# A down projection in four groups of four chunks with seven block products in place of eight

## The chip, the core and the metric

The kernel runs on one core of one Trainium2 chip. The metric is the device time of one execution in microseconds. A core has TensorE (PE, its weight loads as PEld), VectorE (DVE), ScalarE (ACT), GpSimd (POOL) and SyncE (SP), which issues the DMAs. TensorE writes to the eight banks of PSUM.

## What is computed

One layer of a hybrid decoder on 512 tokens of width 1024, all in fp32. The part that matters here is the channel mixer, whose hidden width is 2816, or 22 chunks of 128 channels:

```python
hf = rmsnorm(x, norm_ffn[i])
up = causal_dwconv(hf @ w_up[i], ffn_dw_w[i], ffn_dw_b[i])
gate, val = jnp.split(up, 2, axis=-1)
x = x + (jax.nn.gelu(gate) * val) @ w_down[i]
```

Ahead of it stand a convolution and a sparse attention over a combined projection, merged and projected; behind it a gated embedding and a last norm.

## The kernel before

Every fp32 operand of a large product is cut into a pair of parts, hi (a ScalarE copy, `hi_of`, L107) and lo (a VectorE subtraction, `lo_of`, L110). A product takes three matmuls: hi with hi, hi with lo, lo with hi (L117 to L119 with the weight as stationary operand, L123 to L125 with the activations).

**Weights** come as a stream of 512 KB pieces in their order of use (`pieces`, `Stream`). SyncE loads a piece into one of two buffers (L208); `pump`, which each consumer calls once a piece, starts the cut of pieces that were asked for in an earlier call, up to four pieces ahead (`CUT`). The stages of a cut are put between the matmuls by `work`, so that they stand at a fixed place in the queues of ScalarE and VectorE.

**The channel mixer** goes through the 22 chunks in groups of 8, 8 and 6 (`FFN_GROUPS`). For each chunk f, `up_chunk` (L1161) runs 24 matmuls for the gate half and 24 for the value half, with 128 channels on the partitions and 512 tokens as columns. Behind each half come the depthwise convolution's first tap on ScalarE (L1170) and two on VectorE (L1171, L1172); behind the gate half the gelu (L1180); behind the value half the multiplication (L1182) and the cut of the result into the stationary parts `a` (L107, L110). Then `rows_product` multiplies the group's chunks by w_down: for each column half n and each pair of chunks it takes one piece of weights and runs 4 row tiles of 128 tokens with 2 chunks and 3 matmuls each, into four banks that stay open over the group. At the end of a half, VectorE adds the four banks to the residual `x2` (`residual`, L1137). The chunk pairs come in order, so the chunk that was ready last is used last.

Each engine works its queue in program order, and a DMA queue does too. Nothing but the order of the program and buffers (eight banks of `ps`, eight tiles tagged `act`, four `whl`) decides when something runs.

Of the kernel before, what the change touches and what calls it, by code (L numbers as in the profile page):

```python
# [16 lines left out]
P = 128  # L17
# [24 lines left out]
# heads whose scores, two units ahead, and whose weights, one unit ahead, are due in a unit's steps  # L42
# [41 lines left out]
def block_kernel(ctx: ExitStack, tc: tile.TileContext, x, p, rel_bias, norm_mix, w_in, conv_dw_w, conv_dw_b,  # L84
# [30 lines left out]
    # out += W.T a  with W's parts as the stationary operand  # L115
# [5 lines left out]
    # out += a.T W  with the activations' parts as the stationary operand  # L121
    def mm_a(o, a_hi, a_lo, w_hi, w_lo, start, stop):
        nc.tensor.matmul(o, a_hi, w_hi, start=start, stop=False)  # L123
        nc.tensor.matmul(o, a_hi, w_lo, start=False, stop=False)  # L124
        nc.tensor.matmul(o, a_lo, w_hi, start=False, stop=stop)  # L125

# [1 line left out]
    # A piece lands as fp32 and is cut into an exact (hi, lo) pair of float32r parts, some pieces ahead of its use.  # L128
# [24 lines left out]
    CMP_AFTER = CMP_AT                      # the compression's eight pieces follow the z pieces from this one on  # L153
# [10 lines left out]
    FFN_GROUPS = ((0, 8), (8, 16), (16, NF))  # L164
    for f0, f1 in FFN_GROUPS:
        for f in range(f0, f1):
            for c in (f, NF + f):
                pieces.append((("up", c), [cols(w_up, 0, KC, c * P, P)], KC, P, "whl"))
        if f1 == NF:
            ple_piece(1)  # L170
        rows_pieces("down%d" % f0, w_down, list(range(f0, f1)))
# [4 lines left out]
    class Stream:  # L176
# [6 lines left out]
        def pump(self, force=False):  # L183
            """asks for the next pieces; starts to cut those that were asked for in an earlier call"""
            while self.stages:
                self.work()
            while self.cuts < self.dmas and (force or self.asked[self.cuts] < self.call):
                i = self.cuts
                key, _, a, b, tag = pieces[i]
                if tag is not None:  # L190
                    if tag == "whl" and self.hls >= self.limit:
                        break
                    hl = work("whl", (P, 2, a, b), F32R, tag=tag, bufs=CUT if tag == "whl" else 1)
                    self.hl[i] = hl
                    self.cut(hl, self.raw[i], a)
                    self.hls += tag == "whl"
                    self.raws -= 1
                self.cuts += 1
            while self.dmas < len(pieces):
                i = self.dmas  # L200
                key, srcs, a, b, tag = pieces[i]
                if (self.wholes if tag is None else self.raws) == 2:
# [12 lines left out]

        def cut(self, hl, raw, a):
            """in stages, so that neither engine waits for the other"""
            n = self.parts
            ks = [slice(a * j // n, a * (j + 1) // n) for j in range(n)]
            for j in range(n + 1):  # L220
                def stage(j=j):
                    if j < n:
                        hi_of(hl[:, 0, ks[j]], raw[:, ks[j]])
                    if j:
                        lo_of(hl[:, 1, ks[j - 1]], raw[:, ks[j - 1]], hl[:, 0, ks[j - 1]])
                self.stages.append(stage)
            self.work()
# [18 lines left out]

        def done(self):
# [4 lines left out]

    st = Stream()

# [13 lines left out]
    VNG = ((0, 3), (3, 3), (6, 2))          # row blocks of the values' and branch gates' weights  # L268
# [29 lines left out]
    for _ in range(WARM):                  # keeps the tensor engine's clock up until the first rows are there  # L298
# [3 lines left out]
    class Norm:  # L302
        """RMS norm of one row tile, whose halves may come one after the other."""
# [32 lines left out]
        def to_T(self, hT, t):  # L336
            """-> hT[:, part, kc, tokens]"""
# [9 lines left out]
    def vec_rows(name, parts):  # L347
        """parts: list of [r, 128] APs stacked on partitions -> [128, sum r]."""
# [52 lines left out]
    # relative bias: W[q, h, j] = -bias_h(384 + q - j), +BIG where the distance is negative  # L401
# [7 lines left out]
    # the first tile's norm is shared out, as everything waits for it  # L409
# [75 lines left out]
    KQ = work("KQ", (P, 2, 2, NG, S), F32R, tag="B", bufs=2)   # [(dup d), branch, part, group, token]  # L485
    QQ = work("QQ", (P, NH, S), F32R, tag="B", bufs=2)         # [(part d), head, token]
# [48 lines left out]
    def kpe_evac(kv, o):  # L535
        """the windows' first (ab = 0) and second halves: k[s] + pe[16 ab + s % 16]"""
# [7 lines left out]
    def cmp_x(kv):  # L544
        """Xw[kv][ab][(r d), g, s] = kpe[(g d), s + r]"""
# [68 lines left out]
    def conv_steps():  # L614
        while len(conv_done) < 4 * (CONV_W - 1):
# [3 lines left out]
            # two chains take turns; an instruction then follows one that it doesn't wait for  # L619
# [9 lines left out]
    def conv_tail():  # L629
        """layer norm over channels (on transposed rows), then silu(x) = x/2 (1 + tanh(x/2))"""  # L630
# [71 lines left out]
    def pv_mm(po, v, a, n, start, stop):  # L702
        """po += [v_hi | v_lo].T @ (probabilities, hi and lo part)."""
# [30 lines left out]
    class Unit:  # L734
        """softmax weights of four heads (a group) over one branch's keys, for a tile of queries"""

        def __init__(self, t, g, b):
# [3 lines left out]
            per = min(HPG, 512 // self.nk)              # heads in a tile of 512  # L741
# [78 lines left out]
    def attention(order):  # L820
# [3 lines left out]
        def step(place, fn=None):  # L824
            """one step of the pipeline; fn is run a step later"""
# [7 lines left out]
        def ahead(i):  # L833
            """opens unit i"""
# [65 lines left out]
    class Pace:  # L900
        """runs steps of a generator at a rate, until it ends"""
# [142 lines left out]
    # per-layer embedding rows: p^T parts  # L1044
# [33 lines left out]

# [1 line left out]
    def rows_product(name, ks, a_of, done, late=None, filler=None, between=None, last=None):  # L1080
        """for every row tile t and column half n: done(t, n, psum of a.T @ w[:, half]);
        late(t): what follows a row tile's second half, on the tensor engine after the next tile's product."""
        for n in range(2):
            o = [ps() for _ in range(NT)]
# [61 lines left out]

    gain_f = load_gain(norm_ffn)
    hfT = work("hfT", (P, 2, KC, S), F32R, tag="A", bufs=1)
    hl_ple = st.take("ple", 0)
    for t in range(NT):  # L1150
# [4 lines left out]
                 lambda t: norms[t].to_T(hfT, t), lambda: ple_half(0, hl_ple))  # L1155

# [17 lines left out]

    hpT = gain_p = None
    for f0, f1 in FFN_GROUPS:
        act = {}
# [10 lines left out]
        if f1 < NF:  # L1188
            rows_product("down%d" % f0, ks, a_of, lambda t, n, o: residual(t, n, o, None))
        else:  # L1190
            gain_p = load_gain(norm_ple)
            hpT = work("hpT", (P, 2, KC, S), F32R, tag="A", bufs=1)
            st.pump()
            hl_ple1 = st.take("ple", 1)
            rows_product("down%d" % f0, ks, a_of, lambda t, n, o: residual(t, n, o, gain_p),
                         lambda t: norms[t].to_T(hpT, t), lambda: ple_half(1, hl_ple1))

# [6 lines left out]
    def gate(t, c0, c1, o):  # L1204
        """x2 += sigmoid(o) * ple; ple holds half of it, and sigmoid(x) = (1 + tanh(x/2)) / 2"""
# [21 lines left out]
    def gate_last(hls, o):  # L1227
        """the last tile's second half in two parts, so that less follows the last product"""
# [55 lines left out]
```

## Time and profile before

| what | value |
|---|---|
| median of 3 runs | 837.25 us (836.99 to 838.62) |
| span of the profiled execution | 835.6 us |
| PE busy | 821.3 us, 98% |
| PEld busy | 669.0 us, 80% |
| DVE busy | 539.6 us, 65% |
| ACT busy | 375.4 us, 45% |
| POOL busy | 24.7 us, 3% |
| DMA, mean over the span | 101 GB/s |

The profiled execution's own time is given as its span alone, from its first to its last instruction; the median run is 1.65 us longer, which is what lies around a span. Busy time is the union of an engine's instructions. Matmuls overlap in a pipeline, so the duration of one is longer than its distance to the next; the distance is what a matmul costs. In a timeline row the first two numbers are start and duration, and the brackets at its end hold the engine's idle time before it and what ended it.

### The profile page before, as it was taken

To read this page: it belongs to the slowest core of one execution; us is meant where nothing else is said; L and a number is where in the kernel's file an instruction comes from. 1 tells how busy PE (TensorE), PEld (TensorE's weight loads), DVE (VectorE), ACT (ScalarE), POOL (GpSimd) and SP (SyncE) were. 2 spreads that over 40 slices of the span, in tenths; PEclk is the share of its full clock that TensorE was granted. 3 is DMA by queue.
4 is the path that set the end of the run, shared out by engine and by line. 5 is a ranking of instruction groups with operands and counts; after the bars stand their busy time and mean duration, and the time that the engine had idled before them with its cause. 6 is when DMAs were issued, how large, how long until landed. Compare 5 with 4: busy or idle time off the path is not lost.

```text
span 835.6 us, 10144 instructions
## 1 busy us (share of the span) xinstructions
PE 821.3 (98%) x3872; PEld 669.0 (80%) x3872; DVE 539.6 (65%) x907; ACT 375.4 (45%) x677; POOL 24.7 (3%) x71
## 2 busy tenths in 40 slices
PE   7999999999999999999999999999999999999996
PEld 6888888888888886888788888888888888888885
DVE  6379977988987897935566663355654356655564
ACT  6332524287778874432544441234442123433443
POOL 2000000000010000001000000000000000001012
PEclk9999999999999999999999999999999999999999
DMA  7347787411110116430333324232333323341312
GB/s 217 83 112 202 165 188 173 96 51 51 51 51 27 51 52 219 134 101 26 100 101 102 93 85 125 80 94 81 99 100 102 101 75 102 102 147 55 120 32 101
DMA packets 108026, 84.54 MB, mean 101 GB/s; under 512 B 4080, under 2 KB 93608, under 8 KB 107978
## 3 DMA queue, kind: packets, MB, share of 16 engines
q1 hardware_dynamic: 107978, 83.90, 35.5%
q8 instruction: 30, 0.49, 0.3%
q14 instruction: 18, 0.15, 0.1%
HBM read 79.36 MB, written 2.43 MB: 98 GB/s over the span
## 4 chain that ended last, share of the span: by engine, by line
PE 96%; ACT 1%; DVE 1%; DMA 1%; issue 0%; POOL 0%; SPq 0%; POOLq 0%; ACTq 0%
PE ps L117 19%; PE ps L119 19%; PE ps L118 19%; PE ps L123 9%; PE ps L124 9%; PE ps L125 9%; PE ps L759 2%; PE ps L785 2%; PE ps L565 2%; PE ps L704 1%; PE ps L705 1%; PE ps L341 1%; PE ps L713 1%; DMA vraw<-in_w_in 1%; PE ps L803 0%
## 5 line engine op out<-in xcount | busy, mean ns | idle before, releaser
L110 DVE TENSOR_TENSOR whl<-wraw,whl 128x1024 fp32r<-128x1024 f32 (+1 forms) x159 | 155.6, 987 | 146.8 <-ACT whl L107 143.7
L107 ACT ACTIVATE whl<-wraw 128x1024 fp32r<-128x1024 f32 (+1 forms) x159 | 133.7, 862 | 124.2 <-PE ps L125 94.3
L117 PE MATMUL ps<-hfT,whl 128*128 128x512 f32 x352 | 139.1, 395 | 0.3 <-ACT hfT L107 0.3
L118 PE MATMUL ps<-hfT,whl 128*128 128x512 f32 x352 | 139.1, 395 | 0.2 <-DVE hfT L110 0.2
L119 PE MATMUL ps<-hfT,whl 128*128 128x512 f32 x352 | 139.0, 395 | 0.0
L117 PE MATMUL ps<-hT,whl 128*128 128x512 f32 x256 | 102.8, 402 | 0.0
L119 PE MATMUL ps<-hT,whl 128*128 128x512 f32 x256 | 101.1, 395 | 0.3 <-DVE whl L110 0.3
L118 PE MATMUL ps<-hT,whl 128*128 128x512 f32 x256 | 100.9, 394 | 0.0
L625 DVE SCALAR_TENSOR_TENSOR acc<-aT,convw,acc 128x512 f32<-128x512 f32 x120 | 86.2, 746 | 1.0
L118 PEld LDWEIGHTS ps<-hfT,whl 128*128 128x128 f32 x352 | 66.2, 188 | 16.4 <-DVE hfT L110 0.5
L117 PEld LDWEIGHTS ps<-hfT,whl 128*128 128x128 f32 x352 | 66.2, 188 | 16.2 <-ACT hfT L107 0.5
L119 PEld LDWEIGHTS ps<-hfT,whl 128*128 128x128 f32 x352 | 66.2, 188 | 15.9
L123 PE MATMUL ps<-whl,a 128*128 128x512 f32 x176 | 69.7, 396 | 0.0
L125 PE MATMUL ps<-whl,a 128*128 128x512 f32 x176 | 69.5, 395 | 0.0
L124 PE MATMUL ps<-whl,a 128*128 128x512 f32 x176 | 69.5, 395 | 0.0
L1170 ACT ACTIVATE up<-ps,ffnw 128x512 f32<-128x512 f32 x44 | 34.3, 780 | 61.5 <-PE ps L119 61.5
L1171 DVE SCALAR_TENSOR_TENSOR up<-ps,ffnw,up 128x511 f32<-128x511 f32 x44 | 33.0, 750 | 43.9 <-ACT up L1170 43.8
L119 PEld LDWEIGHTS ps<-hT,whl 128*128 128x128 f32 x256 | 48.2, 188 | 12.0 <-DVE whl L110 0.7
L117 PEld LDWEIGHTS ps<-hT,whl 128*128 128x128 f32 x256 | 48.2, 188 | 9.9 <-issue 0.2
L118 PEld LDWEIGHTS ps<-hT,whl 128*128 128x128 f32 x256 | 48.3, 189 | 9.4
L125 PEld LDWEIGHTS ps<-whl,a 128*128 128x128 f32 x176 | 33.0, 188 | 8.0
L123 PEld LDWEIGHTS ps<-whl,a 128*128 128x128 f32 x176 | 33.1, 188 | 7.9
(191 smaller groups left out, 1263.6 us busy)
## 6 DMA issues: line engine op xcount, KB each, us to landing
wraw<-in_w_up SPq DMA_DIRECT2D x44, 512.0 KB
wraw<-in_w_in SPq DMA_DIRECT2D x32, 512.0 KB
wraw<-in_w_down SPq DMA_DIRECT2D x22, 512.0 KB
wraw<-in_w_out SPq DMA_DIRECT2D x8, 512.0 KB
wraw<-in_w_ple_gate SPq DMA_DIRECT2D x8, 512.0 KB
W<-vdram SPq DMA_DIRECT2D x8, 264.0 KB
xin<-in_x SPq DMA_DIRECT2D x4, 512.0 KB
wraw<-in_w_ck SPq DMA_DIRECT2D x4, 512.0 KB
```

The lines of the kernel that those rows point to most:

```text
L107: nc.scalar.activation(dst, src, AF.Copy, scale=scale)
L110: nc.vector.tensor_tensor(dst, src, f32(hi), op=ALU.subtract)
L117: nc.tensor.matmul(o, hl[:, 0, j, cs], a_hi, start=start, stop=False)
L118: nc.tensor.matmul(o, hl[:, 0, j, cs], a_lo, start=False, stop=False)
L119: nc.tensor.matmul(o, hl[:, 1, j, cs], a_hi, start=False, stop=stop)
L123: nc.tensor.matmul(o, a_hi, w_hi, start=start, stop=False)
L124: nc.tensor.matmul(o, a_hi, w_lo, start=False, stop=False)
L125: nc.tensor.matmul(o, a_lo, w_hi, start=False, stop=stop)
L565: nc.tensor.matmul(hid_ps[kv][hf], raw[:, jj, hf * P:(hf + 1) * P], Xw[kv][j // 8][:, :, s0:s0 + 16 * (NCMP - 1) + 1:16], start=j == 0, st ...
L625: nc.vector.scalar_tensor_tensor(acc[:, c, :], a[:, k:k + S], convw[:, 4 * k + c:4 * k + c + 1], acc[:, c, :], op0=ALU.mult, op1=ALU.add)
L1170: nc.scalar.activation(u, o, AF.Identity, scale=fw(2, c), bias=fw(3, c))
L1171: nc.vector.scalar_tensor_tensor(u[:, 1:], o[:, :S - 1], fw(1, c), u[:, 1:], op0=ALU.mult, op1=ALU.add)
```

## The change

Sixteen of the 22 chunks are now worked in four groups of four; the last group of six is as before. In a group of four the product is taken as two pairs of chunks. For a pair, the activations are a 2 by 2 matrix of blocks (256 tokens by 128 channels) and the weights are one too (128 channels by 512 columns). Seven block products stand in place of eight, by a form of Strassen's scheme that works on sums and differences of blocks.

- `act_pair` collects the two multiplied chunks of a pair in `apair`. GpSimd makes four sums of 256 columns (s1, s3, s2, s4); then ScalarE and VectorE cut four tiles into parts: blocks 11 and 12 (512 columns), block 22 (256), s1 and s3 (512), s2 and s4 (512).
- `Quad` loads a group's four weight blocks (4 DMAs of 512 KB, issued behind the group's last up piece) into one buffer of tag `B`. GpSimd makes the differences t1, t2, t3 (`sums`) and t4 (`last_sum`), 1024 columns each. Seven operands are cut for four chunks, where before four chunks took four pieces.
- `seven_products` runs seven products of 2 row tiles, 2 pairs and 3 matmuls. The first (bank pair m) is copied by ScalarE into a second bank pair, `seeded`, that stays taken from the product with w_out to the last group of four; `seeded` then gathers three more products, and a third pair e takes two. VectorE adds a bank pair to `x2` six times in a group.
- In each product both pairs of chunks are used, the second right behind the first.

```diff
-    FFN_GROUPS = ((0, 8), (8, 16), (16, NF))
+    FFN_GROUPS = ((0, 4), (4, 8), (8, 12), (12, 16), (16, NF))
+    DOWN_OPS = ("11", "t1", "t2", "21", "t3", "22", "t4")
...
+    class Quad:
+        def __init__(self, f0):
+            raw = work("draw", (P, 4, 2, 512), tag="B", bufs=2)
...
+                nc.sync.dma_start(raw[:, i], rows[:, r, :, c * 512:(c + 1) * 512])
...
+        def sums(self):
+            x = work("dsum", (P, 2, 2, 512), tag="accX")
+            self.at["t1"], self.at["t2"], self.at["t3"] = x[:, 0], x[:, 1], self.at["12"]
+            self.sub(x[:, 0], "12", "11")
+            self.sub(x[:, 1], "22", "t1")
+            self.sub(self.at["12"], "22", "12")
+        def last_sum(self):
+            self.at["t4"] = self.at["11"]
+            self.sub(self.at["11"], "21", "t2")
...
+    def act_pair():
+        raw = work("apair", (P, 2, 512), tag="pT", bufs=2)
+        for j in range(2):
+            uv = yield
+            nc.vector.tensor_tensor(raw[:, j], uv[0], uv[1], op=ALU.mult)
...
+        add = lambda to, a, b, op: nc.gpsimd.tensor_tensor(to, a, b, op=op)
+        add(s1, a21, a22, ALU.add)
+        add(s3, a11, a21, ALU.subtract)
+        add(s2, s1, a11, ALU.subtract)
+        add(s4, a12, s2, ALU.subtract)
+        parts = {}
+        for src, names in ((raw[:, :, 0:256], ("11", "12")), (a22.unsqueeze(1), ("22",)), (sums[0], ("s1", "s3")),
+                           (sums[1], ("s2", "s4"))):
+            n = len(names)
+            x_ = work("a", (P, 2, n, 256), F32R, tag="act", bufs=8)
+            hi_of(x_[:, 0], src)
+            lo_of(x_[:, 1], src, x_[:, 0])
...
+        def product(bank, a, b, start):
+            st.pump()
+            hl = st.take("down", f0, b)
+            for tt in range(2):
+                ts = slice(tt * P, (tt + 1) * P)
+                for i, pair in enumerate(pairs):
+                    mm_a(bank[tt], pair[a][:, 0, ts], pair[a][:, 1, ts], hl[:, 0, i, :], hl[:, 1, i, :],
+                         start and i == 0, i == len(pairs) - 1, skip_group_check=True)
+                st.work()
+            st.done()
+        m, e = [ps(), ps()], [ps(), ps()]
+        product(m, "11", "11", True)
+        for tt in range(2):
+            nc.scalar.activation(seeded[tt], m[tt], AF.Copy)
+        product(e, "s1", "t1", True)
+        product(seeded, "s2", "t2", False)
+        add_to(1, 1, e)
+        add_to(0, 1, seeded)
+        product(m, "12", "21", False)
+        add_to(0, 0, m)
+        product(seeded, "s3", "t3", False)
+        add_to(1, 1, seeded)
+        product(e, "s4", "22", False)
+        add_to(0, 1, e)
+        product(seeded, "22", "t4", False)
+        add_to(1, 0, seeded)
```

Two places of the order are shown, both at a group's end. In the rows, `ps` is a bank, `whl` a weight's parts, `a` the parts of activations, `hfT` the up projection's input, and a number behind a name tells buffers apart.

TensorE before, behind the last up chunk of the first group of eight, where `a_3823` and `a_3896` are the group's first two chunks:

```order
L119 MATMUL ps_4303<-hfT_3348,whl_4191 128x512
L123 MATMUL ps_4337<-whl_4226,a_3823 128x512 [waits Activation_49]
L124 MATMUL ps_4337<-whl_4226,a_3823 128x512 [waits DVE_49]
L125 MATMUL ps_4337<-whl_4226,a_3823 128x512
L123 MATMUL ps_4337<-whl_4226,a_3896 128x512
L124 MATMUL ps_4337<-whl_4226,a_3896 128x512
L125 MATMUL ps_4337<-whl_4226,a_3896 128x512
L123 MATMUL ps_4338<-whl_4226,a_3823 128x512
```

TensorE with the change, behind the last up chunk of the first group of four, where `a_3905` holds the first pair's blocks 11 and 12 and `a_4063` those of the second pair:

```order
L119 MATMUL ps_4026<-hfT_3350,whl_3918 128x512
L123 MATMUL ps_4075<-whl_3957,a_3905 128x512 [waits Activation_49]
L124 MATMUL ps_4075<-whl_3957,a_3905 128x512 [waits DVE_49]
L125 MATMUL ps_4075<-whl_3957,a_3905 128x512
L123 MATMUL ps_4075<-whl_3957,a_4063 128x512 [waits Activation_49]
L124 MATMUL ps_4075<-whl_3957,a_4063 128x512
L125 MATMUL ps_4075<-whl_3957,a_4063 128x512 [waits DVE_49]
L123 MATMUL ps_4076<-whl_3957,a_3905 128x512
```

The fourth matmul behind the last up chunk now uses the parts of the pair that this up chunk belongs to; before, it used those of the group's second chunk of eight.

ScalarE with the change at the same place, from the last up chunk's first tap (L1231, L1170 of before) to the first cut behind the copies (`asums` are GpSimd's sums of the second pair, `draw` the weights as loaded, and L1284 the copies into the seeded banks):

```order
L1231 ACTIVATE up_4052<-ps_4026,ffnw1_820 128x512 [waits PE_49]
L107 ACTIVATE a_4063<-apair_3917 128x512 [waits DVE_49]
L107 ACTIVATE a_4066<-apair_3917 128x256
L107 ACTIVATE a_4069<-asums_4057 128x512 [waits Pool_49]
L107 ACTIVATE a_4072<-asums_4058 128x512 [waits Pool_49]
L107 ACTIVATE whl_4079<-draw_3828 128x1024 [waits DMAHW1_49]
L1284 ACTIVATE ps_3346<-ps_4075 128x512 [waits PE_49]
L1284 ACTIVATE ps_3347<-ps_4076 128x512 [waits PE_49]
L107 ACTIVATE whl_4096<-draw_3828 128x1024
```

Before, one cut of `a` stood there and cuts of weights behind it; now two cuts that wait for GpSimd stand ahead of the copies into the seeded banks.

## Rows read from the trace of the kernel before

**Rows 1.** The page: span, and part 1's busy time by engine.

```profile
span 835.6 us, 10144 instructions
PE 821.3 (98%) x3872; PEld 669.0 (80%) x3872; DVE 539.6 (65%) x907; ACT 375.4 (45%) x677; POOL 24.7 (3%) x71
```

**Rows 2.** The page, part 4: the chain that ended last, by engine.

```profile
PE 96%; ACT 1%; DVE 1%; DMA 1%; issue 0%; POOL 0%; SPq 0%; POOLq 0%; ACTq 0%
```

**Rows 3.** Busy us in stretches: 16 up chunks, then the first product.

```profile
core 0: us, PE busy (x) PEld busy (x) DVE busy (x) ACT busy (x) POOL busy (x), PEclk, DMA share, GB/s
404.92:494.00 89.08, 89.08 (x383) 72.26 (x384) 53.36 (x62) 38.28 (x48) 0.00 (x0) 1.00 0.33 95
494.00:538.60 44.60, 44.60 (x193) 35.87 (x192) 17.16 (x19) 9.78 (x10) 0.00 (x0) 1.00 0.34 104
```

**Rows 4.** Timeline, TensorE where the first product begins: start us, duration us.

```profile
494.02 0.40 PE L123 MATMUL ps<-whl,a 128*128 128x512 f32 x1
...
494.71 0.39 PE L123 MATMUL ps<-whl,a 128*128 128x512 f32 x1
...
495.41 0.40 PE L123 MATMUL ps<-whl,a 128*128 128x512 f32 x1
```

**Rows 5.** The same timeline on ScalarE and VectorE, behind the last up chunk.

```profile
494.22 0.78 ACT L1170 ACTIVATE up<-ps,ffnw 128x512 f32<-128x512 f32 x1 [1.55 <-PE ps L119]
...
495.03 0.75 DVE L1171 SCALAR_TENSOR_TENSOR up<-ps,ffnw,up 128x511 f32<-128x511 f32 x1 [1.10 <-ACT up L1170]
...
495.81 0.75 DVE L1172 SCALAR_TENSOR_TENSOR up<-ps,ffnw,up 128x510 f32<-128x510 f32 x1
...
496.60 0.69 DVE L1182 TENSOR_TENSOR up<-up 128x512 f32<-128x512 f32 x1
...
497.32 0.63 ACT L107 ACTIVATE a<-up 128x512 fp32r<-128x512 f32 x1 [2.33 <-DVE up L1182]
...
497.99 0.69 DVE L110 TENSOR_TENSOR a<-up,a 128x512 fp32r<-128x512 f32 x1 [0.70 <-ACT a L107]
```

**Rows 6.** Timeline, TensorE after a wait for a part.

```profile
404.92 0.51 PE L118 MATMUL ps<-hfT,whl 128*128 128x512 f32 x1 [0.23 <-DVE hfT L110]
...
405.26 0.39 PE L119 MATMUL ps<-hfT,whl 128*128 128x512 f32 x1
```

**Rows 7.** Groups by line and shape from 430 us on.

```profile
L110 DVE TENSOR_TENSOR whl<-wraw,whl 128x1024 fp32r<-128x1024 f32 x68 | 83.2, 1224 | 106.0 <-ACT whl L107 105.9
...
L107 ACT ACTIVATE whl<-wraw 128x1024 fp32r<-128x1024 f32 x68 | 71.3, 1051 | 85.0 <-PE ps L125 84.1 <-DMA wraw<-in_w_down 1.0
...
L1137 DVE TENSOR_TENSOR x<-ps,x 128x512 f32<-128x512 f32 x24 | 16.1, 686 | 7.6 <-PE ps L125 7.6
...
L1133 ACT ACTIVATE ple<-ps 128x512 f32<-128x512 f32 x4 | 2.2, 608 | 0.3 <-PE ps L125 0.3
```

**Rows 8.** The same view: a VectorE addition of 256 columns.

```profile
L1209 DVE TENSOR_TENSOR x<-x,pg 128x256 f32<-128x256 f32 x2 | 0.8, 424 | 0.1
```

**Rows 9.** Groups of POOL over the whole span.

```profile
L327 POOL TENSOR_TENSOR rstd<-ss 128x1 f32<-128x1 f32 x16 | 5.7, 353 | 54.1 <-ACT junk L314 53.4 <-ACT junk L1242 0.7
...
L607 POOL MEMSET aT<- 128x30 f32 x4 | 0.4, 116 | 64.8 <-DVE acc L625 64.8
...
L509 POOL MEMSET KCt<- 128x128 f32 x1 | 0.2, 205 | 0.0
```

**Rows 10.** Stretches behind the last matmul, columns as in rows 3.

```profile
828.00:832.00 4.00, 0.00 (x0) 0.00 (x0) 2.40 (x6) 2.05 (x6) 1.37 (x3) 1.00 0.34 126
...
832.40:832.60 0.20, 0.00 (x0) 0.00 (x0) 0.00 (x0) 0.00 (x0) 0.00 (x0) 0.53 0.00 0
```

**Rows 11.** Timeline, TensorE in the first stage: matmuls of 280 columns.

```profile
12.35 0.43 PE L123 MATMUL ps<-vhl,hT 128*128 128x280 f32 x1
...
12.58 0.43 PE L124 MATMUL ps<-vhl,hT 128*128 128x280 f32 x1
```

More of the change, by code (lines that the diff above doesn't have):

```diff
@@ L170, in block_kernel @@
             ple_piece(1)
-        rows_pieces("down%d" % f0, w_down, list(range(f0, f1)))
+        if f1 < NF:
+            quad_pieces(f0)
+        else:
+            rows_pieces("down%d" % f0, w_down, list(range(f0, f1)))
     rows_pieces("gate", w_ple_gate, list(range(KC)))
@@ L189, in pump @@
                 key, _, a, b, tag = pieces[i]
-                if tag is not None:
+                if tag == "quad":
+                    quads[key[1]].sums()
+                elif tag == "op":
+                    if self.hls >= self.limit:
+                        break
+                    hl = work("whl", (P, 2, a, b), F32R, tag="whl", bufs=CUT)
+                    self.hl[i] = hl
+                    self.cut(hl, quads[key[1]].at[key[2]], a)
+                    if key[2] == "11":
+                        self.stages.append(quads[key[1]].last_sum)
+                    self.hls += 1
+                elif tag is not None:
                     if tag == "whl" and self.hls >= self.limit:
@@ L1077, in block_kernel, with rows_product @@
             nc.vector.scalar_tensor_tensor(yT[m][:, 1], ysum[m], 0.5, f32(yT[m][:, 0]), op0=ALU.mult, op1=ALU.subtract)
-    def rows_product(name, ks, a_of, done, late=None, filler=None, between=None, last=None):
+    def rows_product(name, ks, a_of, done, late=None, filler=None, between=None, last=None, banks=None):
         for n in range(2):
-            o = [ps() for _ in range(NT)]
+            o = [banks[t] if n and banks and t < len(banks) else ps() for t in range(NT)]
             def part(t, kk, hl):
@@ L1145, in residual @@
             norms[t].rows()
+    seeded = [ps(), ps()]
     gain_f = load_gain(norm_ffn)
@@ L1154, in block_kernel @@
                  lambda t, n, o: residual(t, n, o, gain_f),
-                 lambda t: norms[t].to_T(hfT, t), lambda: ple_half(0, hl_ple))
+                 lambda t: norms[t].to_T(hfT, t), lambda: ple_half(0, hl_ple), banks=seeded)
     def fw(k, c):
@@ L1173, in up_chunk @@
         return u
+    def act_pair():
[3 more added lines that the diff above has]
+            nc.vector.tensor_tensor(raw[:, j], uv[0], uv[1], op=ALU.mult)
+        sums = [work("asums", (P, 2, 256), tag="S", bufs=8) for _ in range(2)]
+        a11, a21, a12, a22 = (raw[:, j, h * 256:(h + 1) * 256] for j in range(2) for h in range(2))
+        s1, s3, s2, s4 = sums[0][:, 0], sums[0][:, 1], sums[1][:, 0], sums[1][:, 1]
+        add = lambda to, a, b, op: nc.gpsimd.tensor_tensor(to, a, b, op=op)
[10 more added lines that the diff above has]
+            lo_of(x_[:, 1], src, x_[:, 0])
+            for i, name in enumerate(names):
+                parts[name] = x_[:, :, i]
+        yield parts
@@ new lines, in seven_products, with add_to @@
+    def seven_products(f0, pairs):
+        x_ = lambda r, c, tt: x2[:, 2 * r + tt, c * 512:(c + 1) * 512]
+        def add_to(r, c, bank):
+            for tt in range(2):
+                nc.vector.tensor_tensor(x_(r, c, tt), bank[tt], x_(r, c, tt), op=ALU.add)
+        def product(bank, a, b, start):
[10 more added lines that the diff above has]
+        product(m, "11", "11", True)
+        for tt in range(2):
+            nc.scalar.activation(seeded[tt], m[tt], AF.Copy)
[11 more added lines that the diff above has]
+        add_to(1, 0, seeded)
@@ L1175, in block_kernel @@
     hpT = gain_p = None
     for f0, f1 in FFN_GROUPS:
+        if f1 < NF:
+            pairs = []
+            for f in range(f0, f1, 2):
+                pair = act_pair()
+                next(pair)
+                for j in range(2):
+                    ug = up_chunk(f + j)
+                    nc.scalar.activation(ug, ug, AF.Gelu_apprx_tanh)
+                    uv = up_chunk(NF + f + j)
+                    parts = pair.send((ug, uv))
+                pairs.append(parts)
+            st.skip("quad", f0)
+            seven_products(f0, pairs)
+            continue
@@ L1187, in block_kernel @@
         a_of = lambda k, t: (act[k][:, 0, t * P:(t + 1) * P], act[k][:, 1, t * P:(t + 1) * P])
[L1188 to L1196, printed above, removed]
+        gain_p = load_gain(norm_ple)
+        hpT = work("hpT", (P, 2, KC, S), F32R, tag="A", bufs=1)
+        st.pump()
+        hl_ple1 = st.take("ple", 1)
+        rows_product("down%d" % f0, ks, a_of, lambda t, n, o: residual(t, n, o, gain_p),
+                     lambda t: norms[t].to_T(hpT, t), lambda: ple_half(1, hl_ple1))
     gain_o = load_gain(norm_final)
```

28 lines of the change are left out of this document (24 added, 4 removed).

## The prediction

> **What bounds the kernel now.** I read the page's busy shares first, then the chain that ended last, then stretches of the channel mixer, then single rows at the one place where the change alters what TensorE waits for. TensorE is busy for 821.3 of 835.6 us [rows 1] and makes up 96% of the chain that ended last [rows 2]. In the channel mixer it has no hole at all: it is busy for the whole of the 16 up chunks (89.08 us, so 5.57 us a chunk) and for the whole of the first product (44.60 us), while VectorE is busy for 17.16 us of that product, ScalarE for 9.78 and GpSimd for none [rows 3]. So here a matmul less is time less, and any wait of TensorE is time more.
>
> What is a matmul worth? Not its recorded 0.40 us, as these overlap. Six matmuls lie between the starts at 494.02 and 495.41 [rows 4], 0.232 us each, and 44.60 us for the product's 192 matmuls [rows 3] gives the same.
>
> **What the change takes away.** Sixteen chunks took two groups of 192 matmuls, 384. Now each of four groups runs 7 products x 2 row tiles x 2 pairs x 3 matmuls = 84, together 336. That is 48 less: 48 x 0.232 = 11.1 us saved, if nothing else changes.
>
> **What it adds on the path: a wait at each group's start.** Before, a product began with the group's first chunks, and the chunk just finished was used last, over 60 matmuls later. Now the fourth matmul of the first product needs the parts of the second pair, which the last up chunk has only just delivered. How long these parts take can be read off, because the same chain ran before beside the product [rows 5]: first tap on ScalarE from 494.22, second and third tap on VectorE from 495.03 and 495.81, the multiplication from 496.60, hi from 497.32 for 0.63, so until 497.95, lo from 497.99 until 498.68. The new pair tile changes none of these sizes: the tile cut first has 512 columns too. ScalarE and VectorE are idle ahead of this chain in the row (1.55 and 1.10 us), and the change puts nothing more there.
>
> TensorE by these times: three matmuls on the first pair from 494.02, then nothing. The fourth starts when hi is there, at 497.99. A matmul that ends such a wait pushes the next one back: after a wait the distance was 0.34 us (404.92 to 405.26 [rows 6]) in place of 0.232. So the fifth starts at 498.33, the sixth waits for lo until 498.72, and the seventh starts at 499.06, where before the seventh of the product started at 495.41 [rows 4]. The delay is 3.65 us a group, 14.6 us in four.
>
> **What it adds beside the path.** Counted from that start, products two to seven begin at 500.45, 503.2, 506.0, 508.8, 511.6 and 514.4, 2.78 us each.
>
> ScalarE's queue behind hi: the cut of block 22, two cuts of GpSimd's sums, the cut of a weight, two copies into the seeded banks, which the third product needs at 503.2. The copies wait behind the cut of s2 and s4, which waits for four GpSimd sums of 256 columns. No row has such a sum on GpSimd. Below, it is bounded by VectorE's addition of 256 columns, 0.42 us [rows 8]; above, by GpSimd's own addition of one column, 0.353, and three streams of 256 columns at the pace of its memsets, (205 - 116) / 98 columns = 0.9 ns a column [rows 9]: 0.353 + 3 x 0.23 = 1.05 us. I take 0.75, the middle, since neither end is nearer in kind. From the multiplication's end at 497.3, four of them end at 500.45; then 0.63 for the cut, 1.05 for the weight's and 0.61 for a copy [rows 5, 7], which overlap by some 0.07 at each change: the first copy is done at 502.65, 0.55 ahead of need. The cover is gone at 0.90 us a sum, and at 1.05 the third product starts 0.6 us late. The sums s1 and s3, which the second product's fourth matmul needs at 501.15, are early by 1.5 us.
>
> VectorE's queue has no idle time left in a group: behind lo of the pair 0.42 + 2 x 0.69 for the other cuts, seven cuts of weights at 1.22 and twelve additions at 0.69 [rows 5, 7, 8], 18.6 us in 19.5. Step by step, the addition that empties the first seeded bank ends at 508.84, where the fifth product wants that bank at 508.8. So this train runs level with TensorE, and any lateness of it comes through. I charge 0.2 us a group, between 0 (the train as reckoned) and 1.0 (three further links of 0.3).
>
> The weights' differences are off the path: 16 GpSimd additions of 1024 columns, at most 0.353 + 3 x 0.93 = 3.1 us each by the same bound, three of them, 9.4 us, spread over the last three up chunks, 16.7 us. Their loads (four blocks of 512 KB a group, on SyncE's queue ahead of the next group's up pieces) are issued some three chunks, 16.7 us, ahead of the first cut and five, 28 us, ahead of the last; at 104 GB/s [rows 3] the up piece ahead of them and the first block take 10 us, all four 25 us. The three extra cuts a group and the two seeded banks, which leave six for the rest, cost nothing while the up chunks hide them, as VectorE is busy for 53.36 of 89.08 us there [rows 3].
>
> **Sum.** 4 x (3.65 + 0.2) - 11.1 = 15.4 - 11.1 = 4.3 us longer: a span of 839.9 us for 835.6. The median run stands 1.65 us above the profiled span, so I forecast 841.5 us.
>
> **Rivals.**
>
> *GpSimd and VectorE get in each other's way.* While the four sums run, VectorE makes lo of the pair and of block 22 from two SBUF inputs each. No row has GpSimd on more than one column beside such work: it is idle in both stretches [rows 3]. If they take turns, lo of the pair takes 0.69 us longer, on the path: 2.8 us in four groups, 844.3. If GpSimd's chain and VectorE's train slip by 1.1 us more, 4.4 us come on top, 848.7. It decides from a sum of 0.90 us on, or from any lengthening of lo. The Trainium skill speaks for it: "GPSIMD Engine Reference", section "Key points", says that GpSimd shares its SBUF interfaces with VectorE and contends with VectorE instructions that have two SBUF inputs. No run here shows it so far.
>
> *TensorE's clock falls during the wait.* The wait is 3.3 us of idle TensorE. At the end of the kernel the granted clock was still 1.00 over the four idle us from 828 to 832 and had fallen by 832.4 [rows 10], which is 4.5 us behind the last matmul, so the wait should be too short. At the lower level a matmul of 280 columns took 0.23 us (12.35 to 12.58 [rows 11]), the price of 512 columns later, so about half speed. If a wait cost as much again in slow running, half of 3.4 us, four groups would cost 6.8 us: 848.3. The Trainium skill, "TensorE: Matmul & The Clock Gate", section "Part 1: The HAM clock gate", says that idle time sets the clock back to 1.2 GHz; by the row above the trace agrees for a longer gap.
>
> *Faster: a matmul is worth its duration.* If each of the 48 matmuls gave back its recorded 0.40 and not 0.232 us, 19.2 us would go and 15.4 come: 833.4. It decides from 15.4 / 48 = 0.32 us a matmul. Rows 3 and 4 speak against it.
>
> *No change that can be told.* If the wait were 2.4 to 3.2 us a group, as when one of the six links overlaps another by 0.5 to 1.2 us, the sum lies within 1.7 us of zero, about 837.3. Nothing in the rows shows such an overlap, as each link reads what the one before wrote.
>
> **How the numbers follow.** About 0.2% (1.7 us) is what a measurement of this kernel can tell from no change. Chances: the forecast 0.64 (840.7 to 844, from no charge for VectorE's train to sums at their upper bound), the contention 0.14, the clock 0.06, the duration 0.05, no change 0.11. Faster by over 0.2% is the duration's 0.05, the same is 0.11, slower 0.84. The predicted time is the forecast's, 841.5. The range reaches from 838.7, which leaves out the faster case and most of the unchanged one (0.15), to 848.0, which takes in the contention but for its worst end and leaves out the clock.
>
> **What would show it.** TensorE should have four idle gaps of about 3.3 us each, one behind the last up chunk of each group of four, ended by ScalarE's cut of `a`; the distance of matmuls should stay 0.232 us and the granted clock 1.00. The chain that ended last should hold ScalarE and VectorE, at the lines of the taps, the multiplication and the cut, for some 14 us more. GpSimd's sums of 256 columns should take 0.4 to 1.05 us. I would be wrong if the gaps were shorter than 2.8 us (then the product savings win), if TensorE waited for GpSimd or for the seeded banks by over 0.6 us a group, or if lo of the pair took more than 0.75 us.

## The result and the profile after

The changed kernel took 860.53 us (median of 4 runs, 859.85 to 860.86), the kernel before, run beside it on the same chip, 837.12 (836.97 to 838.62): a ratio of 1.0272 [1.0258, 1.0287]. The two medians lie 23.4 us apart; the ratio makes it 22.8 us, and the shares below go by the ratio. The forecast was 4.3 us longer, with a range up to 848.0. The direction was right, the size was off by a factor of five.

The page of the kernel after: span, TensorE's busy time, the granted clock in 40 slices, the chain that ended last by engine, and the group of the first matmul of a product (out<-in, count, busy, mean ns, idle before it and its releaser).

```profile
span 859.1 us, 10235 instructions
...
PE 819.0 (95%) x3824; PEld 666.3 (78%) x3824; DVE 600.7 (70%) x967; ACT 397.2 (46%) x713; POOL 98.9 (12%) x119
...
PEclk9999999999999999999998998999899899999998
...
PE 82%; DVE 8%; ACT 3%; issue 2%; POOL 2%; DMA 1%; SPq 0%; POOLq 0%; ACTq 0%
...
L123 PE MATMUL ps<-whl,a 128*128 128x512 f32 x160 | 67.5, 422 | 24.8 <-ACT a L107 24.8
```

Against [rows 1] TensorE runs 48 matmuls less, as planned, but is busy for only 2.3 us less, and the span is 23.5 us longer. In the chain, TensorE's 96% [rows 2] became 82%; VectorE, ScalarE and GpSimd hold 13%. The 24.8 us of idle time are four waits of 6.2 to 6.3 us, one at the start of each group's products, ended by the cut of `a`. That is the place that the prediction named, at nearly twice the idle time that it gave (3.3 us). And the clock row, which should have stayed at 9, has an 8 wherever such a wait lies (the last 8 is the kernel's end).

The timeline of the kernel after, at one group's end (start us, duration us; idle time and what ended it in brackets):

```profile
450.97 0.40 PE L125 MATMUL ps<-whl,a 128*128 128x512 f32 x1
...
453.39 0.76 ACT L1231 ACTIVATE up<-ps,ffnw 128x512 f32<-128x512 f32 x1
...
454.66 0.74 DVE L1232 SCALAR_TENSOR_TENSOR up<-ps,ffnw,up 128x511 f32<-128x511 f32 x1
455.44 0.75 DVE L1233 SCALAR_TENSOR_TENSOR up<-ps,ffnw,up 128x510 f32<-128x510 f32 x1
456.22 0.69 DVE L1243 TENSOR_TENSOR apair<-up 128x512 f32<-128x512 f32 x1
456.95 0.94 ACT L107 ACTIVATE a<-apair 128x512 fp32r<-128x512 f32 x2 [2.79 <-DVE apair L1243]
456.99 1.90 POOL L1247 TENSOR_TENSOR asums<-apair 128x256 f32<-128x256 f32 x2 [8.30 <-DVE apair L1243]
...
457.63 0.80 PE L123 MATMUL ps<-whl,a 128*128 128x512 f32 x1 [6.26 <-ACT a L107]
458.22 0.63 PE L124 MATMUL ps<-whl,a 128*128 128x512 f32 x1
458.65 0.63 PE L125 MATMUL ps<-whl,a 128*128 128x512 f32 x1
...
461.64 0.49 PE L123 MATMUL ps<-whl,a 128*128 128x512 f32 x1
461.97 0.40 PE L124 MATMUL ps<-whl,a 128*128 128x512 f32 x1
```

From the second tap (454.66) to the cut (456.95), the links and their lengths are those of [rows 5]. But the chain starts late. In [rows 5] the second tap stands 1.01 us behind the start of the first product (495.03 against 494.02); here the first product began at 450.51, so the tap was due at 451.52 and came 3.14 us later. Then, behind the wait, matmuls start 0.43 us apart in place of 0.232, from 458.22 to 461.64.

Stretches of the kernel after around that wait, columns as in [rows 3] (TensorE's clock stands behind POOL's busy time):

```profile
454.50:455.00 0.50, 0.00 (x0) 0.00 (x0) 0.50 (x2) 0.00 (x0) 0.00 (x0) 1.00 0.00 0
455.00:455.50 0.50, 0.00 (x0) 0.00 (x0) 0.46 (x2) 0.00 (x0) 0.00 (x0) 0.51 0.00 0
461.00:461.50 0.50, 0.50 (x2) 0.40 (x2) 0.00 (x0) 0.50 (x2) 0.00 (x0) 0.50 0.00 0
462.00:462.50 0.50, 0.50 (x4) 0.41 (x3) 0.30 (x1) 0.50 (x2) 0.00 (x0) 1.00 0.00 0
```

TensorE had stood idle since 451.4 when the granted clock fell to its lower level (1.2 GHz) at about 455.0, inside the wait; it was back at the upper one by 462.0, with four us of matmuls in between.

So there are two questions: where the chain lost 3.1 us, and what the clock costs. The first is answered half a group earlier. The timeline of the kernel after on GpSimd, VectorE and ScalarE, behind the group's fourth up chunk:

```profile
435.49 2.40 POOL L298 TENSOR_TENSOR dsum<-draw 128x1024 f32<-128x1024 f32 x1
435.56 0.63 ACT L107 ACTIVATE a<-asums 128x512 fp32r<-128x512 f32 x1 [1.40 <-POOL asums L1247]
436.10 1.05 ACT L107 ACTIVATE whl<-wraw 128x1024 fp32r<-128x1024 f32 x1
436.23 2.21 DVE L110 TENSOR_TENSOR a<-asums,a 128x512 fp32r<-128x512 f32 x1 [1.30 <-ACT a L107]
437.05 0.76 ACT L1231 ACTIVATE up<-ps,ffnw 128x512 f32<-128x512 f32 x1
437.97 2.73 POOL L298 TENSOR_TENSOR dsum<-draw,dsum 128x1024 f32<-128x1024 f32 x1
438.37 3.42 DVE L110 TENSOR_TENSOR whl<-wraw,whl 128x1024 fp32r<-128x1024 f32 x1
440.66 3.39 POOL L298 TENSOR_TENSOR draw<-draw 128x1024 f32<-128x1024 f32 x1
441.70 0.74 DVE L1232 SCALAR_TENSOR_TENSOR up<-ps,ffnw,up 128x511 f32<-128x511 f32 x1
...
446.08 0.74 DVE L1232 SCALAR_TENSOR_TENSOR up<-ps,ffnw,up 128x511 f32<-128x511 f32 x1
...
450.30 0.74 DVE L1232 SCALAR_TENSOR_TENSOR up<-ps,ffnw,up 128x511 f32<-128x511 f32 x1
```

Two things happen here. First, ScalarE's tap of the fifth up chunk (437.05) stands behind the cuts of the pair's sums, which wait for GpSimd; it was due 0.2 us behind that chunk's end, at 434.0 (450.51 - 3 x 5.57 + 0.2), and is 3 us late. Second, VectorE's two lo subtractions ahead of the second tap take 2.21 and 3.42 us, where the same shapes took 0.69 and 1.22 [rows 5, 7]. Their ends follow GpSimd's: the first difference ends at 437.89 and the first lo at 438.44; the second difference ends at 440.70 and the second lo at 441.79. And a difference that meets a lo under way is stretched in turn, 2.73 and 3.39 us for 2.40. The second tap itself, from PSUM and one SBUF tile, keeps its 0.74 us beside the third difference.

The second taps of the last four up chunks start at 441.70, 446.08, 450.30 and 454.66. They were due 5.57 us apart, at 434.81, 440.38, 445.95 and 451.52. They are late by 6.9, 5.7, 4.4 and 3.1 us: the engines behind TensorE recover some 1.25 us a chunk, and three chunks are too few.

### The profile page after: what moved, and what is told of

It is laid out like the page before. It is cut to its first block, busy times and chain, and to the rows that moved or that the text cites. A ratio compares the mean times of both kernels' runs of the same rounds, so it can differ in the third digit from the quotient of the medians.

```text
span 859.1 us, 10235 instructions
## 1 busy us (share of the span) xinstructions
PE 819.0 (95%) x3824; PEld 666.3 (78%) x3824; DVE 600.7 (70%) x967; ACT 397.2 (46%) x713; POOL 98.9 (12%) x119
## 4 chain that ended last, share of the span: by engine, by line
PE 82%; DVE 8%; ACT 3%; issue 2%; POOL 2%; DMA 1%; SPq 0%; POOLq 0%; ACTq 0%
PE ps L117 15%; PE ps L119 15%; PE ps L118 15%; PE ps L123 9%; PE ps L124 9%; PE ps L125 9%; DVE whl L110 3%; PE ps L817 2%; PE ps L843 2%; DVE up L1233 2%; POOL asums L1247 2%; PE ps L623 2%; DVE up L1232 2%; PE ps L762 1%; PE ps L399 1%
## 5 line engine op out<-in xcount | busy, mean ns | idle before, releaser
L110 DVE TENSOR_TENSOR whl<-wraw,whl 128x1024 fp32r<-128x1024 f32 (+1 forms) x143 | 144.7, 1022 | 88.2 <-ACT whl L107 87.5
L107 ACT ACTIVATE whl<-wraw 128x1024 fp32r<-128x1024 f32 (+1 forms) x143 | 117.0, 842 | 88.8 <-PE ps L125 41.5
L123 PE MATMUL ps<-whl,a 128*128 128x512 f32 x160 | 67.5, 422 | 24.8 <-ACT a L107 24.8
L124 PE MATMUL ps<-whl,a 128*128 128x512 f32 x160 | 66.2, 414 | 0.0
L125 PE MATMUL ps<-whl,a 128*128 128x512 f32 x160 | 66.0, 413 | 0.0
L1231 ACT ACTIVATE up<-ps,ffnw 128x512 f32<-128x512 f32 x44 | 34.0, 773 | 55.7 <-PE ps L119 55.7
L123 PEld LDWEIGHTS ps<-whl,a 128*128 128x128 f32 x160 | 32.3, 202 | 33.7 <-ACT a L107 26.6
L119 PEld LDWEIGHTS ps<-hT,whl 128*128 128x128 f32 x256 | 48.2, 188 | 12.1 <-DVE whl L110 0.7
L125 PEld LDWEIGHTS ps<-whl,a 128*128 128x128 f32 x160 | 31.8, 199 | 8.3 <-DVE a L110 0.9
```

The costliest lines, as they stand in the source:

```text
L107: nc.scalar.activation(dst, src, AF.Copy, scale=scale)
L110: nc.vector.tensor_tensor(dst, src, f32(hi), op=ALU.subtract)
L119: nc.tensor.matmul(o, hl[:, 1, j, cs], a_hi, start=False, stop=stop)
L123: nc.tensor.matmul(o, a_hi, w_hi, start=start, stop=False, **kw)
L124: nc.tensor.matmul(o, a_hi, w_lo, start=False, stop=False, **kw)
L125: nc.tensor.matmul(o, a_lo, w_hi, start=False, stop=stop, **kw)
```

## Experiments

The theory was: VectorE and ScalarE come late out of the middle of the group because of GpSimd's differences, and the longer wait then drops the clock. The rivals were that the wait at the group's end alone, or GpSimd's sums, or VectorE's load by itself, explains the time. Each edit is against the changed kernel. Times are medians beside runs of the kernel before on the same chip.

### What the clock costs

Unused matmuls fill the wait of the first product (the edit's main lines):

```diff
...
                 for i, pair in enumerate(pairs):
+                    if idle and tt == 0 and i == 1:
+                        spare = ps()
+                        for _ in range(idle):
+                            nc.tensor.matmul(spare, pairs[0][a][:, 0, ts], hl[:, 0, 0, :], start=True, stop=True)
...
```

With 18 of them:

> 18 matmuls that nothing uses (4.2 us) stand in the wait, between the third and the fourth matmul of each group's first product; the output is not touched. Theory (the wait of 6.2 us is set by VectorE's and ScalarE's chain, and TensorE then works at the lower clock for some ten matmuls, about 2 us a group): the clock stays at 1.00, the wait ends when it did, and the time falls by 4 x 2 = 8 us, to about 852.5 us. Rival (the clock has no part in it; TensorE would wait as long anyway for something else): 860.5 us or more.

It took 856.44 us, 1.0226 [1.0211, 1.0241], more than the 852.5 expected: 2.0 to 2.1 us of idle time were left in each group. The clock fell behind the first and the third of these waits and held behind the second and the fourth. The stretches behind the first (2.02 us idle, until 457.02) and the second (2.08 us, until 529.40):

```profile
457.60:460.90 3.30, 3.30 (x8) 2.48 (x8) 1.69 (x3) 1.20 (x3) 2.62 (x3) 0.50 0.02 5
529.40:532.70 3.30, 3.29 (x13) 2.43 (x14) 2.28 (x3) 0.89 (x2) 3.22 (x4) 1.00 0.00 0
```

So this run does not give the clock's whole cost. With a longer fill, 25 matmuls:

> As e1_fill, but 25 matmuls that nothing uses (5.8 us), since in e1_fill some 2 us were still idle and the clock fell again. Theory: idle stretches of under 1 us, the clock stays at 1.00, and all 8.4 us of slow running go: 851 to 853 us. Rival (the clock falls with any wait): 856 us.

It took 854.46 us, 1.0201 [1.0186, 1.0216]; 851 to 853 had been expected. A stretch of it around the first wait, columns as in [rows 3]:

```profile
449.00:465.00 16.00, 15.50 (x65) 11.67 (x64) 10.81 (x14) 8.29 (x12) 3.85 (x4) 1.00 0.01 2
```

The clock stays at 1.00. By the two ratios, slow running costs 0.0071 of 837 us, some 6 us in place of the 8.4 reckoned, and 16.8 us over the kernel before are left.

### What the differences cost

All of GpSimd's differences of weights are left out, so that the products use the loaded blocks:

```diff
...
-            self.sub(x[:, 0], "12", "11")
-            self.sub(x[:, 1], "22", "t1")
-            self.sub(self.at["12"], "22", "12")
...
+            self.at["t1"], self.at["t2"] = self.at["12"], self.at["21"]
...
-            self.sub(self.at["11"], "21", "t2")
```

> GpSimd's 16 differences of weights are left out (blocks of w_down are cut in their place), so the output is another; all cuts, products and additions stay. Theory (a VectorE instruction with two SBUF inputs and a GpSimd instruction take turns, and the 1024-column differences set VectorE back by some 3 us that it still lags at the group's end): the wait falls from 6.2 to about 3.5 us a group, the clock mostly stays, time 840 to 845 us. Rival (the four sums of 256 columns at 1 us each, which ScalarE's and VectorE's queues wait for, make the lag): 853 us or more.

It took 847.41 us, 1.0120 [1.0105, 1.0135], above the 840 to 845 expected and below the rival's 853. VectorE's cuts of the up weights from 400 to 770 us, in the kernel after and then here:

```profile
L110 DVE TENSOR_TENSOR whl<-wraw,whl 128x1024 fp32r<-128x1024 f32 x47 | 66.3, 1410 | 32.6 <-ACT whl L107 32.1
```

```profile
L110 DVE TENSOR_TENSOR whl<-wraw,whl 128x1024 fp32r<-128x1024 f32 x50 | 61.2, 1223 | 39.7 <-ACT whl L107 39.3
```

The mean is back at 1223 ns, that of [rows 7]. The waits of TensorE in the same run (us in total, times, longest), and stretches around the first of them:

```profile
PE ps L123 <- ACT a L107: 12.5, 4, 3.1
```

```profile
450.50:452.50 2.00, 0.00 (x0) 0.00 (x0) 1.93 (x3) 0.00 (x0) 0.00 (x0) 1.00 0.00 0
452.50:453.00 0.50, 0.00 (x0) 0.00 (x0) 0.19 (x1) 0.27 (x1) 0.16 (x1) 0.63 0.00 0
453.00:459.00 6.00, 5.59 (x13) 4.41 (x14) 3.66 (x5) 3.54 (x7) 3.63 (x4) 0.50 0.00 0
```

Without the differences the wait is 3.1 us, close to the 3.3 that the prediction worked out from [rows 5]; the 3 us that ScalarE's tap loses to the sums are recovered by the group's end. But the clock falls at this wait as well, at about 452.6, where it had been expected mostly to stay. So the same was run with 12 unused matmuls in the wait:

> As e2_no_differences (GpSimd's differences of weights left out, so the output is another), with 12 matmuls that nothing uses (2.8 us) in the wait of 3.1 us. Theory (the change's time is the forecast's sum and two things on top, VectorE's lag and the clock): with both away the forecast's sum is left, 837.4 + 14.0 of waits - 11.1 = about 839 to 841 us. Rival (something else costs too): 844 us or more.

It took 842.56 us, 1.0057 [1.0042, 1.0072]: 4.8 us over the kernel before, without lag and without a fall of the clock, between the 839 to 841 expected and the rival's 844. Within the 1.3 us that the ratio leaves open, this is the prediction's sum, 4.3, measured by itself. The three ratios share the 22.8 us out: 4.8 for the terms that the prediction had, 12.1 for the differences (1.0201 - 1.0057), 6 for the clock (1.0272 - 1.0201); the last two are uncertain by some 1.8 us each.

### Sums, smaller instructions, another engine

The four sums of a pair are left out; the parts are cut from blocks of `apair` in their place:

```diff
-        add(s1, a21, a22, ALU.add)
-        add(s3, a11, a21, ALU.subtract)
-        add(s2, s1, a11, ALU.subtract)
-        add(s4, a12, s2, ALU.subtract)
...
```

> GpSimd's 32 sums of activations are left out (blocks of the activations are cut in their place), so the output is another; the differences of weights stay. Theory: VectorE's lag comes mostly from the differences, but the wait for the sums stands ahead of it in the queue and shifts the differences against the cuts; a wait of 4.5 to 6 us a group, 848 to 857 us. Rival (the sums make the lag): about 842 us.

852.29 us, 1.0175 [1.0158, 1.0192]. The four waits add up to 17.1 us in place of 24.8, 4.3 to 4.4 each. ScalarE's tap of the fifth chunk is 1 us late here in place of 3, the differences run earlier, and VectorE's lo subtractions beside them are still lengthened: four of `a` together take 5.88 us mid-group and 2.23 at the group's end, where no difference runs. So the sums set part of the lag, about 2 us a group, but only because the differences come on top: without the differences, and with the sums, the wait was 3.1.

Each difference as four instructions of 256 columns:

```diff
-            nc.gpsimd.tensor_tensor(to, self.at[a], self.at[b], op=ALU.subtract)
+            for k in range(2):
+                for h in range(2):
+                    cs = slice(256 * h, 256 * h + 256)
+                    nc.gpsimd.tensor_tensor(to[:, k, cs], self.at[a][:, k, cs], self.at[b][:, k, cs], op=ALU.subtract)
```

> Each difference of weights is made by four GpSimd instructions of 256 columns in place of one of 1024. Theory (turns by whole instructions): a VectorE instruction waits for at most one short instruction, so its lag falls below 2 us; wait 4 to 5.5 us a group, 845 to 855 us. Rival (both slow down in proportion while they overlap, whatever the size): 858 to 863 us.

850.69 us, 1.0156 [1.0141, 1.0171]; the waits are 15.0 us. The timeline at the same place as above:

```profile
435.27 4.27 POOL L301 TENSOR_TENSOR dsum<-draw 128x256 f32<-128x256 f32 x4
...
437.19 1.75 DVE L110 TENSOR_TENSOR whl<-wraw,whl 128x1024 fp32r<-128x1024 f32 x1
...
438.86 0.74 DVE L1235 SCALAR_TENSOR_TENSOR up<-ps,ffnw,up 128x511 f32<-128x511 f32 x1
439.50 2.84 POOL L301 TENSOR_TENSOR dsum<-draw,dsum 128x256 f32<-128x256 f32 x4
```

The work on GpSimd is the same, and it takes longer there: four pieces take 2.84 us where VectorE has next to no two-input work (from 439.50), and 4.27 us beside such work (from 435.27), where the whole took 2.40. Yet the lo that took 3.42 us takes 1.75, and from the first difference's start to the fifth chunk's second tap 3.6 us pass in place of 6.2. What VectorE waits for is thus the one GpSimd instruction under way, and its length is what counts. The Trainium skill, "SBUF — State Buffer", section "Who interferes with whom", says just this of a VectorE instruction with two SBUF inputs and a GpSimd instruction that reads SBUF: the port pair that they share is an exclusive lock, and the one that comes second is held up until the first is done. The trace agrees, in both directions: 3.42 us for 1.22 on VectorE, 3.39 for 2.40 on GpSimd.

The differences on VectorE, so that nothing is shared:

```diff
-            nc.gpsimd.tensor_tensor(to, self.at[a], self.at[b], op=ALU.subtract)
+            nc.vector.tensor_tensor(to, self.at[a], self.at[b], op=ALU.subtract)
```

> The differences of weights are made on VectorE in place of GpSimd; the order of the products is that of the change. Theory: no turns with GpSimd, but three differences of some 1.2 us each stand in VectorE's queue in a row, so it lags by 1 to 3 us at the group's end; wait 4 to 6 us, 845 to 857 us. Rival (GpSimd's slowness and not the sharing was the cost): 842 us.

859.88 us, 1.0271 [1.0254, 1.0288]: no better, and outside what was expected. The timeline of it at the same place:

```profile
435.80 1.22 DVE L298 TENSOR_TENSOR dsum<-draw 128x1024 f32<-128x1024 f32 x1
437.05 1.23 DVE L298 TENSOR_TENSOR dsum<-draw,dsum 128x1024 f32<-128x1024 f32 x1
438.19 1.22 DVE L298 TENSOR_TENSOR draw<-draw 128x1024 f32<-128x1024 f32 x1
...
440.46 0.74 DVE L1232 SCALAR_TENSOR_TENSOR up<-ps,ffnw,up 128x511 f32<-128x511 f32 x1
```

Three differences now cost VectorE 3.7 us in its own queue, ahead of the same tap. In the kernel after, it lost 1.5 + 2.2 = 3.7 us there to turns. The waits come out alike, 25.1 us for 24.8. So the cost is not peculiar to the two engines' sharing: whatever holds VectorE for 3.7 us in the middle of a group of four comes through at its end.

### Where the wait can go

The group's products are moved behind the first up chunk of the next group, so that TensorE has work while the last pair is made:

```diff
-            seven_products(f0, pairs)
+            pending.append([AFTER_UPS, f0, pairs])
...
+    def up_then(c):
+        u = up_chunk(c)
+        if pending:
+            pending[0][0] -= 1
+            if pending[0][0] == 0:
+                seven_products(*pending.pop()[1:])
+        return u
```

The pieces of the stream move with them. With `AFTER_UPS = 1`:

> Each group's seven products stand behind the next group's first up chunk (5.57 us of TensorE) in place of right behind its own last one; the same instructions otherwise. Theory (only the chain behind the last up chunk, 3.65 us plus some 2.6 us of VectorE's lag, is uncovered): a wait of 0 to 1.5 us a group, no fall of the clock, and the 11.1 us of removed matmuls show: 827 to 833 us, faster than the kernel before. Rival (the lag moves along, since GpSimd and VectorE take turns in the product too, and TensorE waits for it elsewhere): 837 us or more.

835.63 us, 0.9974 [0.9964, 0.9985]: faster than both kernels, but less so than expected. With 2:

> The same behind the next group's second up chunk (11.1 us of cover). Theory: no wait at the group's start; 826 to 829 us. Rival (the lag moves along): 837 us or more.

839.07 us, 1.0019 [1.0010, 1.0028], no faster than the kernel before, as the rival had it. In both, TensorE's wait for `a` is gone from the list of its waits and another is there. With 1, then with 2:

```profile
PE ps L123 <- ACT ps L1291: 6.6, 4, 1.7
```

```profile
PE ps L123 <- ACT ps L1291: 7.9, 4, 2.0
```

The third product waits for the copies into the seeded banks. They stand in ScalarE's queue behind the cut of s2 and s4, which waits for the four GpSimd sums, and behind the cut of a weight. The prediction had named 0.90 us a sum as the point from which this wait comes. The four sums take 3.93 us here, 0.98 each: those that start while VectorE's cut of the same pair is under way are held up, as the differences are. Stretches of both around the first wait, again with 1, then with 2:

```profile
461.03:462.67 1.64, 0.00 (x0) 0.00 (x0) 1.60 (x3) 1.64 (x4) 0.00 (x0) 1.00 0.00 0
462.67:470.00 7.33, 7.26 (x30) 5.69 (x31) 7.33 (x9) 4.48 (x5) 0.00 (x0) 1.00 0.00 0
```

```profile
467.24:469.10 1.86, 0.00 (x0) 0.00 (x1) 1.82 (x3) 1.86 (x4) 0.00 (x0) 1.00 0.00 0
469.50:472.50 3.00, 3.00 (x8) 2.33 (x8) 3.00 (x4) 1.95 (x3) 0.00 (x0) 0.50 0.00 0
```

After 1.64 us of idle time the clock held, after 1.86 it fell; the other three waits of each execution went the same way as its first. The second execution is the slowest of its ten (841.68 us, mean granted clock 0.989). The ten have a median clock of 0.993, for 0.997 with 1, and 0.004 of 838 us is 3.4 us: by this estimate the falls of the clock account for most of the 3.4 us between the two versions.

Then the copies were put ahead of the weight's cut:

```diff
-        product(m, "11", "11", True)
+        product(m, "11", "11", True, pump=False)
         for tt in range(2):
             nc.scalar.activation(seeded[tt], m[tt], AF.Copy)
+        st.pump()
```

> As e6_later1, with the copies into the seeded banks ahead of the cut of weights that stood before them on ScalarE. Theory (in e6_later1 the third product waits 1.65 us a group for the copies, which stand behind GpSimd's sums, two cuts and a tap): the wait falls to 0 to 0.7 us, 829 to 833 us. Rival (VectorE's train then holds the fifth product by as much): 835 us.

836.12 us, 0.9980 [0.9970, 0.9989]: no gain over 835.63, as the rival had it. The timeline shows why, the third and the fifth product of a group:

```profile
462.24 0.50 PE L123 MATMUL ps<-whl,a 128*128 128x512 f32 x1 [0.70 <-ACT ps L1292]
...
469.12 0.47 PE L123 MATMUL ps<-whl,a 128*128 128x512 f32 x1 [1.03 <-DVE x L1275]
```

The wait for the copies went from 1.65 to 0.70 us, and 1.03 us for VectorE's addition to `x2` took its place: VectorE's train, with no slack as the prediction had reckoned it, is next. The theory was that it is late by what it lost to GpSimd, so two edits were joined, this one and the pieces of 256 columns:

> As e10_copy_first, with each difference of weights in four GpSimd instructions of 256 columns. Theory (VectorE's lag at the group's end falls by some 2 us, so the copies come earlier by as much): no wait at the third product, 827 to 830 us. Rival: as e10_copy_first.

829.59 us, 0.9905 [0.9888, 0.9921], with the same clock as the kernel before (0.997). The page and TensorE's only wait in a product:

```profile
span 827.5 us, 10283 instructions
...
PE 810.5 (98%) x3824; PEld 659.9 (80%) x3824; DVE 589.1 (71%) x967; ACT 396.3 (48%) x713; POOL 111.7 (13%) x167
```

```profile
PE ps L123 <- DVE x L1278: 2.7, 4, 0.7
```

The wait for the copies is gone, though the sums are as long as before, so it came from the lag as well as from the sums. This version is 8.2 us faster than the kernel before. Of the 11.1 us that 48 matmuls are worth, 2.7 are still lost to that wait; 11.1 - 2.7 = 8.4.

## Why the prediction was off

- **48 matmuls at 0.232 us, 11.1 us saved: right.** The distance of matmuls is 0.232 us where the clock is up, and the last version gets 8.2 us with 2.7 us of waits left.
- **A wait of 3.65 us at each group's start: right as a term, and not the whole.** With the differences out of the way the idle time was 3.1 us a group, and the sum that rests on it, 4.3, measured 4.8 with the clock kept up.
- **"The weights' differences are off the path": this step failed.** Their own duration was bounded well (2.40 us beside nothing, 3.39 at most, for 3.1). What failed was to ask only when they must be done. They hold up VectorE's two-input work by 3.7 us in the middle of a group. Price: 12.1 us.
- **"cost nothing while the up chunks hide them, as VectorE is busy for 53.36 of 89.08 us": the reason behind it failed.** The idle 40% is not slack that can be used at once. The work behind an up chunk is a chain across ScalarE and VectorE, in queue order, and it recovers only about 1.25 us a chunk (late by 6.9, 5.7, 4.4, 3.1). Three chunks lay between the disturbance and the group's end. The same sentence hid ScalarE's 3 us behind the sums, which did get absorbed, as long as nothing else came.
- **The contention rival (0.14) had the right pair of engines and the wrong place.** It was looked for at the group's end, beside the four sums, and priced at 2.8 to 7.2 us. There the two engines do hold each other up (the sums took 0.72 to 1.22 us), but lo of the pair kept its 0.69 us, and without the differences the time lies within 0.5 us of the sum that has no such term. The long instructions run mid-group, where the prediction had not looked for their neighbours in VectorE's queue.
- **"so the wait should be too short": this step failed.** One row, the kernel's end [rows 10], was taken as the rule for the clock: it held for four idle us there. In these runs it fell at every wait of 6.2 and of 3.1 us, at all four of 1.9 to 2.0 us in one execution, at two of four of 2.0 to 2.1 us in another, and held at those of 1.6. The rival's price was sound: 6.8 us reckoned, 6 measured. Even with no lag the clock falls, and the run that shows that case, 847.41, lies near the rival's 848.3. Its chance of 0.06 was the error.
- **Sums of 256 columns at 0.75 us: right for one alone, not for the four.** Pieces of that size that meet no two-input VectorE work took 0.73 to 0.75 us. The sums took 0.72, 1.22, 0.91 and 1.06 at the group's end above, 0.98 on average, as VectorE's cuts beside them hold them up; the term had no such hold-up in it. In the kernel after, this stands behind the wait for `a`. Where the products are moved, the copies wait behind these sums and behind the lag together.
- **VectorE's train at 0.2 us a group: not seen by itself in the kernel after,** where TensorE waits in the products for `a` alone. It shows once that wait is gone, with 1.0 and 0.7 us a group in the last two versions.

## What to carry to other kernels

A share of busy time is no cover for new work on an engine that is one link of a chain: put the new instruction into the queue at its place, move the chain behind it, and count how many rounds the chain has to recover before somebody waits. Long GpSimd instructions beside two-input VectorE work cost VectorE up to their own length, so cut them small; that another place in the order would help too is likely, but was not tried. Where a change gives TensorE a new idle time of some microseconds, put a fall of the clock into the sum and not among the remote rivals, and where possible let the next stage's matmuls fill the wait.

## What the runs showed of the hardware that was not expected

- The granted clock fell after an idle stretch of 1.86 us and held after 1.64; of four stretches of 2.0 to 2.1 us in one execution it fell behind two and held behind two; and at the end of the kernel before it held for four [rows 10]. The length of the idle stretch alone does not tell whether it falls.
- A GpSimd addition of 256 columns took 0.73 to 0.75 us where it met no two-input VectorE work, and one of 1024 columns 2.40. From 0.74 and 2.40, (2.40 - 0.74) / 768 = 2.2 ns a column and some 0.2 us that do not depend on the size, by estimate.
- VectorE's instructions with one input from PSUM and one from SBUF kept their 0.74 us beside a running GpSimd instruction, and those with two SBUF inputs took up to 3.2 times theirs (2.21 us for 0.69).
